# A gated-recurrence and retention layer: the next half's h and the out-projection's tiles loaded into their own slots and split there, and a reordered release of the result banks

## Chip, cores and metric

One NeuronCore of a Trainium2 chip runs the whole layer as one launch. The metric is the device time of one execution in microseconds (us), lower is better; the figure that is compared is the median of several executions.

## Reference

One layer over 2048 positions of width 1024, in float32. All large products are dense; the two mixers are run chunk by chunk.

```
mod = silu(c) @ w_ada + b_ada ;  shift, scale, gate = split(mod)
h    = rms_norm(x, norm_g) * (1 + scale) + shift                     # 2048 x 1024
proj = h @ w_in                                                      # 1024 -> 9216
hq, hf, hi, hz, rq, rk, rv, rz, ga, gb = split(proj)
uA = head_rms_norm(HGRN2(silu(hq), f(hf), hi)) * silu(hz)            # 8 heads of 128
uB = head_rms_norm(Retention(rotary(rq), rotary(rk), rv)) * silu(rz) # 8 heads, key 64, value 128
m  = sigmoid(ga) * uA + sigmoid(gb) * uB
x  = x + gate * (m @ w_out)
out = rms_norm(x, final_g)
```

## The kernel before

The sequence is handled in two halves of 1024 positions (`sb` 0 and 1), each of two blocks of 512 (`tb`). The projection is cut into 72 "quads" (36 for each half, listed in `ORDER`): a quad is 256 columns of w_in for the 1024 positions of a half. A quad is made by seven block products instead of eight (a Strassen form): product `m` = 1 to 7 multiplies one combination of the four 512 x 512 quarters of h (named A11, A12, A22, S1, S2, S3, S4 in `combos`) with one combination of the weights, as 4 steps of three 128x128 by 128x512 matmuls. The three come from a split of each float32 operand into a high part (rounded to fp32r) and the rest: `split_into` lets ScalarE (ACT) copy the source into the first half of a tile and VectorE (DVE) subtract that copy from the source into the second half.

TensorE (PE) runs in the order of the program. `product_order` interleaves quad n = i+1 with the end of quad i: (2,n) (7,i) (1,n) (5,n) (4,i) (3,n) (6,n). Each quad owns one result bank, `x0` or `x1` by its parity; the sums of 2 and 5, 3 go through `y` (in the same bank) and `v`, which ACT copies out (`stash`, lines L477). (4,i) ends a quad, and its result is left in the quad's bank, where `take_a` (a gate's sigmoid, L571), `take_v` (a transpose on DVE, L588), `take_b` (rotary products, L639 to L642) or `take_g` (sigmoid L680 and product L685) read it. Not until they have done so can the product (2, n+1), or the transposes `turned_u` that put the mixers' output in the same bank, begin. `meet` (L703) multiplies the gate with those transposes.

The other engines' order is set by a list scheduler: program order, except that work inside `tc.high_priority(offset=...)` is ranked that many instructions earlier. Each engine then takes its instructions strictly in the order written. All DMAs of the loop but the weights (ACT's queue) and the rotary tables (GpSimd's) are issued by SyncE's queue (SP), also in order.

Tiles and slots that matter here: `tmp` hands out scratch tiles of 128x512 (tag "tp", `NTP` = 4 slots) to everything short-lived. `a_tile` hands out the 28 (`NA`) tiles of tag "A"; in the loop these are the seven combinations of h by four row tiles, and in the last part w_out and m.

Beside the loop runs work in small steps, put between products by `Background`: `tree`, `hgrn_out` and `retention` (the mixers); and, as a side thread that gets a step about once a product, `next_h`. It computes h for the second half (statistics, then x transposed times scale and shift), stores it to memory, loads it back four tiles at a time, forms the four sums (`combine`, L301 to L307, in place) and stores all seven combinations (L1062). At the end of the first half `change_h` loads each combination into a scratch tile (L1072), takes an A tile and splits it. `NEXT` says after which products its steps stand.

At the end `load_wo` loads w_out, multiplies it by the gate (L1244) and splits it into A tiles (L295, L296), `out_m` does the same with m, `meet_last` does the last gate, and `out_half` makes 24 matmuls for 128 positions and 512 columns (`ops`).

Of the kernel before, what the change touches and what calls it, by code (L numbers as in the profile page):

```python
# [32 lines left out]
NBW = 3  # L33
NR = 5
NCC = 5
NTP = 4
NQP = 3
NVH = 2
GAP = 8.0
# [23 lines left out]
def tile_hybrid(ctx: ExitStack, tc: tile.TileContext, a: dict, out: bass.AP):  # L63
# [41 lines left out]
        return t  # L105

    NC = 4 * NBLK
    msk = cpool.tile([P, 4, NC, 16], U8, name="msk", tag="msk")
    dmsk = cpool.tile([P, NC, 2], U8, name="dmsk", tag="dmsk")

    def late_consts():
        m32 = upool.tile([P, 512], I32, name="m32", tag="tp", bufs=NTP)
        nc.sync.dma_start(out=m32[:, 0:66], in_=a["msk"])
        G.tensor_copy(
            out=msk, in_=m32[:, 0:64].rearrange("p (l t) -> p l t", l=4).unsqueeze(2).broadcast_to([P, 4, NC, 16])
        )
# [29 lines left out]

    ng = const("ng", [P, KT], a["ng_t"])
    bad = const("bad", [P, 2 * KT], a["bada_t"])
    lg = const("lg", [P, 2 * H], a["lb_t"])
    lb = cpool.tile([P, H], F32, name="lb", tag="lb")  # L150
    omlb = cpool.tile([P, H], F32, name="omlb", tag="omlb")
    nomlb = cpool.tile([P, H], F32, name="nomlb", tag="nomlb")
# [30 lines left out]

    ad = cpool.tile([P, NC, 32], F32, name="ad", tag="ad")
    G.memset(ad, 0.0)
    junk = cpool.tile([P, P], mybir.dt.bfloat16, name="junk", tag="junk")

    mT_dram = [dram(f"mT{sb}_{b}", [H, P, BLK]) for sb in range(NSB) for b in range(NBLK)]

# [104 lines left out]
    def split_into(t, src):  # L294
        S.activation(out=t[0], in_=src, func=AF.Copy)  # L295
        return V.tensor_tensor(out=t[1], in0=src, in1=t[0], op=ALU.subtract)  # L296

    def combine(h11, h12, h21, h22, use):
        for nm, t in (("A11", h11), ("A12", h12), ("A22", h22)):
# [180 lines left out]
    def after(m, q):  # L480
        with tc.high_priority(offset=PEV):
            if m == 2:
                c2s[q] = stash(f"c2_{q}", yb.pop(q))
                return
            if m == 5:
                c5s[q] = stash(f"c5_{q}", vb[q])
                return
            if m == 1:
                t = c2s.pop(q)
                V.tensor_tensor(out=t, in0=xb[q], in1=t, op=ALU.add)  # L490
                got = (0, 0, t)
            elif m == 3:
                c5s[q, 3] = stash(f"c53_{q}", vb.pop(q))
                return
            elif m == 6:
                t = c5s.pop((q, 3))
                V.tensor_tensor(out=t, in0=t, in1=xb[q], op=ALU.subtract)  # L497
                got = (1, 0, t)
            elif m == 7:
                t = c5s.pop(q)  # L500
                V.tensor_tensor(out=t, in0=t, in1=xb[q], op=ALU.subtract)
                got = (1, 1, t)
            else:
                got = (0, 1, xb.pop(q))
        deliver(q, *got)

    def xtag(q):
# [192 lines left out]
    def meet(sb, h, s, tb, g):  # L700
        b = sb * NBLK + tb
        u = mus.pop((h, s, tb))
        V.scalar_tensor_tensor(  # L703
            out=u, in0=g, scalar=gnt[:, s * H + h : s * H + h + 1], in1=uts.pop((h, s, tb)), op0=ALU.mult, op1=ALU.mult
        )
# [14 lines left out]
    def tree(h, sb, f, k, q):  # L720
# [15 lines left out]
        for li in range(7):  # L736
# [49 lines left out]
                )  # L786
            if m < 16:
                V.copy_predicated(  # L788
                    out=ad.rearrange("p c (n two m) -> p (c n) two m", two=2, m=m)[:, :, 1, :],
                    mask=msk[:, li].rearrange("p c (n m) -> p (c n) m", m=m),  # L790
                    data=ps[:, 0 : 16 * NC].rearrange("p (n m) -> p n m", m=m),
                )
# [29 lines left out]
    def normed(pos, dsts, nm, eps=None):  # L822
        n = len(pos)
        ss = upool.tile([P, 2], F32, name=f"ss{nm}", tag="ss", bufs=4)
        rr = upool.tile([P, 2], F32, name=f"rr{nm}", tag="rr", bufs=4)
        for i in range(n):
            S.activation(out=junk, in_=pos[i], func=AF.Square, accum_out=ss[:, i : i + 1])  # L827
        rstd_of(rr[:, 0:n], ss[:, 0:n], P, eps)
        for i in range(n):
            S.activation(out=dsts[i], in_=pos[i], func=AF.Copy, scale=rr[:, i : i + 1])  # L830
# [188 lines left out]
    def next_h(sb):  # L1019
# [30 lines left out]
                htd[tb, kt] = dram(f"hT{b}_{kt}", [P, 512])  # L1050
                nc.sync.dma_start(out=htd[tb, kt], in_=x)
        for j in range(4):
            hs = []
            for tb, kt in ((0, j), (0, 4 + j), (1, j), (1, 4 + j)):
                hs.append(tmp(f"hT{tb}_{kt}"))
                nc.sync.dma_start(out=hs[-1], in_=htd[tb, kt])
            yield
            yield

            def keep(nm, src):  # L1060
                t = hsd[sb, nm, j] = dram(f"hs{sb}_{nm}_{j}", [P, 512])
                nc.sync.dma_start(out=t, in_=src)  # L1062

            combine(*hs, keep)
            yield
            yield

    def change_h(sb):
        for nm in ("A12", "S1", "A11", "S4", "S2", "S3", "A22"):
            for j in range(4):  # L1070
                x = tmp(f"hl{sb}_{nm}_{j}")
                nc.sync.dma_start(out=x, in_=hsd[sb, nm, j])  # L1072
                t = combos[sb, nm, j] = a_tile(f"{nm}_{sb}_{j}")
                split_into(t, x)
                yield


# [156 lines left out]
    def load_wo():  # L1234
        take("f", 1)
        both = upool.tile([P, 1024], F32, name="gates", tag="f", bufs=1)
        for nh in range(2):
            gate[nh] = both[:, nh * 512 : (nh + 1) * 512]
            nc.sync.dma_start(out=gate[nh], in_=gated[nh])
            for kt in range(KT):  # L1240
                w = tmp(f"wr{kt}_{nh}")
                nc.sync.dma_start(out=w, in_=a["w_o"][kt // 2, nh][:, kt % 2, :])
                t = wod[kt, nh] = a_tile(f"wo{kt}_{nh}")
                V.tensor_tensor(out=w, in0=w, in1=gate[nh], op=ALU.mult)  # L1244
                split_into(t, w)
                yield

    def out_m(t):
        mts[t] = []
        for q4 in range(2):  # L1250
            mr = tmp(f"mr{t}_{q4}")
            nc.sync.dma_start(
                out=mr.rearrange("p (k t) -> p k t", t=P),
                in_=mT_dram[t // 4][4 * q4 : 4 * q4 + 4, :, (t % 4) * P : (t % 4 + 1) * P].rearrange("k p t -> p k t"),
            )
            m = a_tile(f"m{t}_{q4}")
            split_into(m, mr)
            mts[t].append(m)

    def out_half(t, nh):  # L1260
# [4 lines left out]
        xh = [xts[t][:, i * 512 : (i + 1) * 512] for i in range(2)]  # L1265
        ss = sss[t]
        fg = pro["fg"]
        ps = bank(f"ops{t}_{nh}", ("x0", "x1", "v")[pro["n"] % 3])
        pro["n"] += 1
        for kt in range(KT):  # L1270
            hi, lo = mts[t][kt // 4]
# [40 lines left out]
    for i in range(2, len(seq)):  # L1312
# [20 lines left out]
        if q == NQ - 1:  # L1333
            if m == 1:
                pro["w"] = load_wo()
            if m in (1, 3, 6, 7):
                some(pro["w"], {1: 4, 3: 4, 6: 4, 7: 4}[m])
            if m == 4:
                pro["fg"] = apool.tile([P, 1024], F32, name="fg", tag="A", bufs=NA)
                nc.sync.dma_start(out=pro["fg"], in_=a["fg"].broadcast_to([P, 1024]))  # L1340
                V.tensor_scalar(
                    out=pro["fg"], in0=pro["fg"], scalar1=float(D) ** 0.5, scalar2=None, op0=ALU.mult
                )
                out_m(0)
        product(i)

    meet_last()
    pro["n"] = 0
    T0 = 2
    order = [(t, nh) for nh in range(2) for t in range(T0)] + [(t, nh) for t in range(T0, L // P) for nh in range(2)]  # L1350
    nm = 1
    for t, nh in order:
        while nm < min(t + 3, L // P):
            if nm == CH:
                bg.drain()
# [103 lines left out]
```

## Time and profile before

| what | value |
|---|---|
| median of 3 executions | 2226.56 us (2220.96 to 2232.41) |
| the profiled execution | 2225.14 us, its span 2223.3 us |
| granted TensorE clock, mean | 0.95 |
| busy share of the span: PE, PE weight load, DVE, ACT, GpSimd | 90%, 72%, 64%, 45%, 12% |
| moved by DMA | 263.10 MB, 118 GB/s |

The views read below: the list of waits ("engine line <- what released it: us in total, times, longest us"), the timeline (start, duration, engine, line, what is written and read, count; in square brackets how long the engine was idle before, and what ended that), and the chain of work that ended last (start, duration, what). `y L70 <- vt L588` reads: PE stood before a matmul into y until DVE's transpose of line 588 had ended.

### The profile page before, as it was taken

How to read it: one execution, taken by the hardware profiler on the slowest of the kernel's cores; microseconds unless marked ns; L12 is line 12 of the kernel's file. 1: busy time of each engine (PE TensorE's matmuls, PEld its weight loads, DVE VectorE, ACT ScalarE, POOL GpSimd, SP SyncE). 2: the span in 40 equal slices, each digit the busy share in tenths (PEclk: the TensorE clock that was granted, in tenths of full speed). 3: DMA queues.
4: the chain of work that ended last, by engine and by line, in shares of the span. 5: the costliest groups of instructions: out<-in, count | busy, mean ns of one | idle time of the engine just before them, and what ended most of it. 6: DMA issues, size and time to landing. Idle time of an engine off the chain costs nothing.

```text
span 2223.3 us, 40029 instructions
## 1 busy us (share of the span) xinstructions
PE 1998.1 (90%) x15108; PEld 1611.3 (72%) x15108; DVE 1421.4 (64%) x2677; ACT 1002.2 (45%) x2434; POOL 275.5 (12%) x514
## 2 busy tenths in 40 slices
PE   4889899999998688889789899998999899898998
PEld 2667688777776566678668688776777778686887
DVE  5876666676756466656776767665766676568333
ACT  5624445544464353444535444544454345444232
POOL 1002110211021100210001210211021101210000
PEclk8999899999999899989899899999999999899999
DMA  8154424342344437624444424342354423234443
GB/s 282 35 117 120 121 59 118 95 117 78 103 137 135 128 104 211 205 78 126 140 100 122 124 73 104 93 124 85 83 145 124 123 76 103 89 107 152 133 150 115
DMA packets 454849, 263.10 MB, mean 118 GB/s; under 512 B 171905, under 2 KB 406401, under 8 KB 454657
## 3 DMA queue, kind: packets, MB, share of 16 engines
q1 hardware_dynamic: 288480, 176.04, 28.0%
q10 hardware_dynamic: 153120, 76.04, 12.0%
q0 software_dynamic: 13056, 8.47, 1.5%
q8 instruction: 119, 1.95, 0.4%
q14 instruction: 74, 0.60, 0.1%
HBM read 188.03 MB, written 72.35 MB: 117 GB/s over the span
## 4 chain that ended last, share of the span: by engine, by line
PE 40%; DVE 9%; DMA 9%; ACT 4%; issue 3%; POOL 2%; SPq 1%; ACTq 0%; DVEq 0%; POOLq 0%
PE x L70 15%; PE ops L70 8%; PE v L70 8%; PE y L70 4%; DVE b L296 2%; PE poh L70 1%; ACT b L295 1%; DMA w<-in_w_b_dram 1%; PE lv L70 1%; DMA sn<-lin 1%; DMA w<-in_w_d_dram 1%; DVE w L416 1%; PE uT L73 1%; PE rt L70 1%; POOL rrh L177 1%
## 5 line engine op out<-in xcount | busy, mean ns | idle before, releaser
L296 DVE TENSOR_TENSOR b<-w,b 128x512 fp32r<-128x512 f32 (+1 forms) x553 | 346.4, 635 | 328.0 <-ACT b L295 318.2
L295 ACT ACTIVATE b<-w 128x512 fp32r<-128x512 f32 (+1 forms) x553 | 316.7, 583 | 356.9 <-PE x L70 265.9
L70 PE MATMUL v<-S,b 128*128 128x512 f32 x1704 | 432.1, 403 | 20.7 <-ACT c L477 14.1
L70 PE MATMUL x<-A,b 128*128 128x512 f32 x1704 | 430.3, 401 | 5.1 <-ACT c L477 3.8
L70 PE MATMUL x<-S,b 128*128 128x512 f32 x1704 | 433.0, 403 | 0.8 <-DVE c L497 0.8
L70 PEld LDWEIGHTS v<-S,b 128*128 128x128 f32 x1704 | 323.1, 193 | 93.2 <-ACT c L477 16.7
L70 PEld LDWEIGHTS x<-A,b 128*128 128x128 f32 x1704 | 322.5, 192 | 73.8 <-ACT c L477 4.2
L70 PEld LDWEIGHTS x<-S,b 128*128 128x128 f32 x1704 | 322.6, 193 | 67.8 <-DVE c L497 1.2
L70 PE MATMUL y<-A,b 128*128 128x512 f32 x840 | 218.4, 411 | 40.1 <-DVE vt L588 32.3
L416 DVE TENSOR_TENSOR w<-w,w 128x512 f32<-128x512 f32 x284 | 194.7, 686 | 80.3 <-DMA w<-in_w_b_dram 26.8
L70 PEld LDWEIGHTS y<-A,b 128*128 128x128 f32 x840 | 163.1, 198 | 77.0 <-issue 36.1
L70 PE MATMUL ops<-wo,m 128*128 128x512 f32 x768 | 176.3, 392 | 0.0
L70 PEld LDWEIGHTS ops<-wo,m 128*128 128x128 f32 x768 | 145.5, 190 | 30.4
L174 POOL TENSOR_SCALAR ssh<-ssh 128x1 f32<-128x1 f32 x128 | 41.8, 327 | 847.8 <-ACT junk L827 844.6
L477 ACT ACTIVATE c<-v 128x512 f32<-128x512 f32 x142 | 84.3, 594 | 115.7 <-PE v L70 98.3
L70 PEld LDWEIGHTS lv<-q,k 128*32 128x32 f32 (+1 forms) x5888 | 71.9, 111 | 43.7 <-issue 30.2
L830 ACT ACTIVATE uh<-poh,rrh 128x128 f32<-128x128 f32 x128 | 47.1, 368 | 123.3 <-POOL rrh L177 123.3
L497 DVE TENSOR_TENSOR c<-c,x 128x512 f32<-128x512 f32 x71 | 48.7, 686 | 80.7 <-PE x L70 80.3
L70 PE MATMUL lv<-q,k 128*32 128x16 f32 (+2 forms) x5888 | 83.3, 189 | 18.4 <-DVE ad L788 6.4
L776 DVE TENSOR_TENSOR q<-q,f 128x512 f32<-128x512 f32 x112 | 76.8, 685 | 19.6 <-PE lv L70 19.5
L477 ACT ACTIVATE c<-y 128x512 f32<-128x512 f32 x70 | 41.7, 596 | 98.4 <-PE y L70 98.4
L177 POOL TENSOR_TENSOR rrh<-ssh,mhalf 128x1 f32<-128x1 f32 x128 | 82.8, 647 | 10.5
(191 smaller groups left out, 2444.4 us busy)
## 6 DMA issues: line engine op xcount, KB each, us to landing
w<-in_w_d_dram ACTq DMA_DIRECT2D x128, 256.0 KB
w<-in_w_c_dram ACTq DMA_DIRECT2D x66, 256.0 KB
mu<-ud SPq DMA_DIRECT2D x64, 256.0 KB
w<-in_w_a_dram ACTq DMA_DIRECT2D x60, 256.0 KB
wa<-in_w_ada_dram SPq DMA_DIRECT2D x16, 512.0 KB
w<-in_w_b_dram ACTq DMA_DIRECT2D x32, 256.0 KB
vd<-vt SPq DMA_DIRECT2D x128, 64.0 KB
vh<-vd SPq DMA_DIRECT2D x64, 128.0 KB
```

The costliest lines, as they stand in the source:

```text
L70: return tc.keep_in_program_order(nc.tensor.matmul(**kw))
L73: return tc.keep_in_program_order(nc.tensor.transpose(**kw))
L174: G.tensor_scalar(out=ss, in0=ss, scalar1=n * EPS, scalar2=None, op0=ALU.add)
L177: G.tensor_tensor(out=dst, in0=ss, in1=mhalf.broadcast_to([P, w]), op=ALU.pow)
L295: S.activation(out=t[0], in_=src, func=AF.Copy)
L296: return V.tensor_tensor(out=t[1], in0=src, in1=t[0], op=ALU.subtract)
L416: V.tensor_tensor(out=out, in0=x, in1=y, op=ALU.add)
L477: S.activation(out=t, in_=ps, func=AF.Copy)
L497: V.tensor_tensor(out=t, in0=t, in1=xb[q], op=ALU.subtract)
L776: V.tensor_tensor(out=qv, in0=qv, in1=tv[:, :, :, 0:1].broadcast_to([P, NU, nb, m]), op=ALU.mult)
L830: S.activation(out=dsts[i], in_=pos[i], func=AF.Copy, scale=rr[:, i : i + 1])
```

## The change

1. `change_h` and `out_m` load straight into the second half of the A tile (seen as float32) and split there: ACT copies to the first half, DVE subtracts in place (`split_here`). No scratch tile is used, and the DMA now waits for the A tile to be free, in SP's queue.
2. `next_h` no longer stores A11, A12 and A22 again: `change_h` reads them from where h was first stored. The four sums are made one load after another, with two scratch tiles at first and one more for each sum, over 8 steps instead of 4 for each of four groups.
3. `NTP` goes from 4 to 5. The space comes from a mask kept once instead of eight times (`msk`, broadcast when it is read, L788), a bf16 scratch row that is dropped (`junk`; ACT's square of L827 writes the destination tile instead), and a constant that borrows another tile's slot.
4. The reading of (4,i)'s result (`deliver` for m = 4) and the product in `meet` move inside `tc.high_priority`, by 600 instructions.
5. At the end: m's first two tiles are loaded at products 6 and 7 of the last quad rather than at and after product 4; the first `out_half` stands before `meet_last`; the result banks are taken in the order x0, v, x1. `load_wo` takes the A tile before the scratch tile.

```
-NTP = 4
+NTP = 5
...
+    def split_here(t):
+        raw = t[1].bitcast(F32)
+        S.activation(out=t[0], in_=raw, func=AF.Copy)
+        V.tensor_tensor(out=t[1], in0=raw, in1=t[0], op=ALU.subtract)
...
             else:
-                got = (0, 1, xb.pop(q))
+                deliver(q, 0, 1, xb.pop(q))
+                return
         deliver(q, *got)
...
-        V.scalar_tensor_tensor(
-            out=u, in0=g, scalar=gnt[...], in1=uts.pop((h, s, tb)), op0=ALU.mult, op1=ALU.mult
-        )
+        with tc.high_priority(offset=PEV):
+            V.scalar_tensor_tensor(... the same ...)
...
-                    mask=msk[:, li].rearrange("p c (n m) -> p (c n) m", m=m),
+                    mask=msk[:, li].rearrange("p (n m) -> p n m", m=m).unsqueeze(1).broadcast_to([P, NC, 16 // m, m]),
...
-            S.activation(out=junk, in_=pos[i], func=AF.Square, accum_out=ss[:, i : i + 1])
+            S.activation(out=dsts[i], in_=pos[i], func=AF.Square, accum_out=ss[:, i : i + 1])
...
         for j in range(4):                                          # next_h
-            hs = []
-            for tb, kt in ((0, j), (0, 4 + j), (1, j), (1, 4 + j)):
-                hs.append(tmp(f"hT{tb}_{kt}"))
-                nc.sync.dma_start(out=hs[-1], in_=htd[tb, kt])
-            yield
-            yield
...
-            combine(*hs, keep)
+            for nm, at in (("A11", (0, j)), ("A12", (0, 4 + j)), ("A22", (1, 4 + j))):
+                hsd[sb, nm, j] = htd[at]
...
+            h22, h21 = load(1, 4 + j), load(1, j)
             yield
+            yield
+            V.tensor_tensor(out=h22, in0=h21, in1=h22, op=ALU.subtract)
+            keep("S1", h22)
+            h11 = load(0, j)
+            yield
+            yield
+            V.tensor_tensor(out=h21, in0=h11, in1=h21, op=ALU.subtract)
+            keep("S3", h21)
+            V.tensor_tensor(out=h11, in0=h22, in1=h11, op=ALU.subtract)
+            keep("S2", h11)
+            yield
+            h12 = load(0, 4 + j)
+            yield
+            yield
+            V.tensor_tensor(out=h12, in0=h12, in1=h11, op=ALU.add)
+            keep("S4", h12)
             yield
...
-                x = tmp(f"hl{sb}_{nm}_{j}")                         # change_h
-                nc.sync.dma_start(out=x, in_=hsd[sb, nm, j])
                 t = combos[sb, nm, j] = a_tile(f"{nm}_{sb}_{j}")
-                split_into(t, x)
+                nc.sync.dma_start(out=t[1].bitcast(F32), in_=hsd[sb, nm, j])
+                split_here(t)
...
-            mr = tmp(f"mr{t}_{q4}")                                 # out_m
+            m = a_tile(f"m{t}_{q4}")
             nc.sync.dma_start(
-                out=mr.rearrange("p (k t) -> p k t", t=P),
+                out=m[1].bitcast(F32).rearrange("p (k t) -> p k t", t=P),
...
-            m = a_tile(f"m{t}_{q4}")
-            split_into(m, mr)
+            split_here(m)
...
+            if m in (6, 7):
+                out_m(m - 6)
             if m in (1, 3, 6, 7):
-                some(pro["w"], {1: 4, 3: 4, 6: 4, 7: 4}[m])
+                some(pro["w"], 4)
...
-                out_m(0)                                            # was at m == 4
         product(i)
...
-    meet_last()
...
-    nm = 1
+    nm = 2
     for t, nh in order:
+        if (t, nh) == (1, 0):
+            meet_last()
```

What the scheduler makes of it. DVE, where h's sums for the second half are made (`hT`, from L301) and a value tile is transposed out of the bank x (`vt`, reading `x`); before:

```order
L416 TENSOR_TENSOR w_1_8654<-w_1_8654,w_3_8725 128x512
L301 TENSOR_TENSOR hT_4_8642<-hT_0_8640,hT_4_8642 128x512
L303 TENSOR_TENSOR hT_0_8640<-hT_0_8636,hT_0_8640 128x512
L305 TENSOR_TENSOR hT_0_8636<-hT_4_8642,hT_0_8636 128x512
L307 TENSOR_TENSOR hT_4_8638<-hT_4_8638,hT_0_8636 128x512
L588 STREAM_TRANSPOSE vt_7_0_1_8685<-x_8362 128x512
L581 TENSOR_TENSOR q_0_8606<-c_29_8720,sg_0_1_0_8762 128x512
```

The same place on DVE in the changed kernel (L592 is the transpose, L1074 the first sum):

```order
L294 TENSOR_TENSOR b_30_8682<-w_2_8582,b_30_8682 128x512
L592 STREAM_TRANSPOSE vt_7_0_1_8680<-x_8361 128x512
L294 TENSOR_TENSOR b_29_8704<-w_1_8436,b_29_8704 128x512
L1074 TENSOR_TENSOR hT_4_8635<-hT_0_8637,hT_4_8635 128x512
L500 TENSOR_TENSOR c_29_8702<-c_29_8702,x_8578 128x512
```

The transpose moved ahead of the sums, and of the weights' split and the sum before them; the four sums no longer stand in a row.

ACT at the change from the first half to the second (`S_1`, `A_1`: copies of the new combinations; `sz`: sigmoid of the last gate, read from bank x); before:

```order
L295 ACTIVATE S_1_1_10608<-hl_S_1_10606 128x512
L571 ACTIVATE sg_1_0_0_10644<-c_36_10560 128x512
L401 DMA w_3_10739<-in_w_c_dram 128x4x128
L295 ACTIVATE S_1_2_10613<-hl_S_2_10611 128x512
L295 ACTIVATE S_1_3_10618<-hl_S_3_10616 128x512
L573 ACTIVATE f_1_10640<-sg_1_0_0_10644,lb,omlb 128x512
L576 ACTIVATE k_1_10641<-sg_1_0_0_10644,omlb,nomlb 128x512
L295 ACTIVATE A_1_0_10668<-hl_A_0_10666 128x512
L680 ACTIVATE sz_7_1_10708<-x_10368 128x512
```

And now:

```order
L298 ACTIVATE S_1_3_10568<-S_1_3_10568 128x512
L404 DMA w_2_10576<-in_w_c_dram 128x4x128
L575 ACTIVATE sg_1_0_0_10595<-c_36_10519 128x512
L404 DMA w_0_10639<-in_w_c_dram 128x4x128
L480 ACTIVATE c_36_10615<-v_10599 128x512
L293 ACTIVATE b_36_10633<-w_0_10385 128x512
L577 ACTIVATE f_1_10591<-sg_1_0_0_10595,lb,omlb 128x512
L580 ACTIVATE k_1_10592<-sg_1_0_0_10595,omlb,nomlb 128x512
L684 ACTIVATE sz_7_1_10655<-x_10339 128x512
L293 ACTIVATE b_37_10659<-w_2_10576 128x512
L298 ACTIVATE A_1_0_10617<-A_1_0_10617 128x512
```

All copies of the S combinations now stand ahead of the copy of the result bank v (L480), and `sz` stands ahead of the first copy of A22.

PE at the end of the last quad (`uT` are the transposes of `meet_last`, `ops` the out-projection); before:

```order
L70 MATMUL x_20116<-A_1_3_10683,b_71_20253 128x512 x3
L73 MATMUL uT_0_1_20341<-ident,mu_7_3_20088 128x128 x4
L70 MATMUL ops_0_20371<-wo_0_20094,m_0_20316 128x512 x3
L70 MATMUL ops_0_20371<-wo_0_20100,m_0_20316 128x512 x3
L70 MATMUL ops_0_20371<-wo_0_20106,m_0_20316 128x512 x3
```

And now, after eight rows of `ops_0_20305` (24 matmuls), of which the last three are shown:

```order
L70 MATMUL ops_0_20305<-wo_0_20129,m_1_20179 128x512 x3
L70 MATMUL ops_0_20305<-wo_0_20135,m_1_20179 128x512 x3
L70 MATMUL ops_0_20305<-wo_0_20141,m_1_20179 128x512 x3
L73 MATMUL uT_0_1_20334<-ident,mu_7_3_20035 128x128 x4
L70 MATMUL ops_0_20352<-wo_0_20039,m_0_20228 128x512 x3
```

One block of the out-projection passed the transposes; everything else on PE stands as before.

More of the change, by code (lines that the diff above doesn't have):

```diff
@@ L107, in tile_hybrid @@
     NC = 4 * NBLK
-    msk = cpool.tile([P, 4, NC, 16], U8, name="msk", tag="msk")
+    msk = cpool.tile([P, 4, 16], U8, name="msk", tag="msk")
     dmsk = cpool.tile([P, NC, 2], U8, name="dmsk", tag="dmsk")
@@ L113, in late_consts @@
         nc.sync.dma_start(out=m32[:, 0:66], in_=a["msk"])
-        G.tensor_copy(
-            out=msk, in_=m32[:, 0:64].rearrange("p (l t) -> p l t", l=4).unsqueeze(2).broadcast_to([P, 4, NC, 16])
-        )
+        G.tensor_copy(out=msk, in_=m32[:, 0:64].rearrange("p (l t) -> p l t", l=4))
         G.tensor_copy(out=dmsk, in_=m32[:, 64:66].unsqueeze(1).broadcast_to([P, NC, 2]))
@@ L148, in tile_hybrid @@
     bad = const("bad", [P, 2 * KT], a["bada_t"])
-    lg = const("lg", [P, 2 * H], a["lb_t"])
+    lg = upool.tile([P, 256], F32, name="lg", tag="dT", bufs=1)[:, 0 : 2 * H]
+    nc.sync.dma_start(out=lg, in_=a["lb_t"])
     lb = cpool.tile([P, H], F32, name="lb", tag="lb")
@@ L185, in tile_hybrid @@
     G.memset(ad, 0.0)
-    junk = cpool.tile([P, P], mybir.dt.bfloat16, name="junk", tag="junk")
     mT_dram = [dram(f"mT{sb}_{b}", [H, P, BLK]) for sb in range(NSB) for b in range(NBLK)]
@@ L702, in meet @@
         u = mus.pop((h, s, tb))
-        V.scalar_tensor_tensor(
-            out=u, in0=g, scalar=gnt[:, s * H + h : s * H + h + 1], in1=uts.pop((h, s, tb)), op0=ALU.mult, op1=ALU.mult
-        )
+        with tc.high_priority(offset=PEV):
+            V.scalar_tensor_tensor(
+                out=u, in0=g, scalar=gnt[:, s * H + h : s * H + h + 1], in1=uts.pop((h, s, tb)), op0=ALU.mult,
+                op1=ALU.mult,
+            )
         if (h, b) not in half:
@@ L788, in tree @@
                 V.copy_predicated(
-                    out=ad.rearrange("p c (n two m) -> p (c n) two m", two=2, m=m)[:, :, 1, :],
-                    mask=msk[:, li].rearrange("p c (n m) -> p (c n) m", m=m),
-                    data=ps[:, 0 : 16 * NC].rearrange("p (n m) -> p n m", m=m),
+                    out=ad.rearrange("p c (n two m) -> p c n two m", two=2, m=m)[:, :, :, 1, :],
+                    mask=msk[:, li].rearrange("p (n m) -> p n m", m=m).unsqueeze(1).broadcast_to([P, NC, 16 // m, m]),
+                    data=ps[:, 0 : 16 * NC].rearrange("p (c n m) -> p c n m", c=NC, m=m),
                 )
@@ L1052, in next_h, with load @@
         for j in range(4):
-            hs = []
-            for tb, kt in ((0, j), (0, 4 + j), (1, j), (1, 4 + j)):
-                hs.append(tmp(f"hT{tb}_{kt}"))
-                nc.sync.dma_start(out=hs[-1], in_=htd[tb, kt])
-            yield
-            yield
+            for nm, at in (("A11", (0, j)), ("A12", (0, 4 + j)), ("A22", (1, 4 + j))):
+                hsd[sb, nm, j] = htd[at]
+            def load(tb, kt):
+                x = tmp(f"hT{tb}_{kt}")
+                nc.sync.dma_start(out=x, in_=htd[tb, kt])
+                return x
             def keep(nm, src):
@@ L1240, in load_wo @@
             for kt in range(KT):
+                t = wod[kt, nh] = a_tile(f"wo{kt}_{nh}")
                 w = tmp(f"wr{kt}_{nh}")
                 nc.sync.dma_start(out=w, in_=a["w_o"][kt // 2, nh][:, kt % 2, :])
-                t = wod[kt, nh] = a_tile(f"wo{kt}_{nh}")
                 V.tensor_tensor(out=w, in0=w, in1=gate[nh], op=ALU.mult)
@@ L1267, in out_half @@
         fg = pro["fg"]
-        ps = bank(f"ops{t}_{nh}", ("x0", "x1", "v")[pro["n"] % 3])
+        ps = bank(f"ops{t}_{nh}", ("x0", "v", "x1")[pro["n"] % 3])
         pro["n"] += 1
```

## The prediction

> **What bounds the kernel now.** I read the page first, then PE's list of waits, then the timeline at each long wait, and the chain for what follows a wait.
>
> ```profile
> span 2223.3 us, 40029 instructions
> PE 1998.1 (90%) x15108; PEld 1611.3 (72%) x15108; DVE 1421.4 (64%) x2677; ACT 1002.2 (45%) x2434; POOL 275.5 (12%) x514
> ```
>
> PE is the bound: it is idle for 2223.3 - 1998.1 = 225 us in all, and the change leaves its instructions as they are but for one block at the end. So the change is worth what it takes from, or adds to, that idle time. The list of waits says what ends it:
>
> ```profile
> PE y L70 <- DVE vt L588: 32.3, 4, 10.1
> PE uT L73 <- DVE sz L685: 22.7, 6, 9.6
> PE uT L73 <- ACT c L477: 22.6, 16, 3.0
> ...
> PE v L70 <- ACT c L477: 14.1, 8, 5.2
> ...
> PE rb L70 <- POOL dgr L1037: 9.9, 3, 5.1
> ...
> PE y L70 <- ACT sg L571: 6.1, 1, 6.1
> ...
> PE v L70 <- DVE mu L703: 2.6, 1, 2.6
> ...
> PE y L70 <- DVE ro L641: 1.6, 1, 1.6
> ```
>
> Five of these rows (vt, sz, sg, mu, ro) are the reading of (4,i)'s bank or `meet`, which the change ranks earlier: 32.3 + 22.7 + 6.1 + 2.6 + 1.6 = 65.3 us in 13 waits. The rest (c, rb and smaller) it does not aim at. Where the long ones stand, from PE's timeline:
>
> ```profile
> 134.21 2.04 PE L70 MATMUL y<-A,b 128*128 128x512 f32 x4 [10.11 <-DVE vt L588]
> ...
> 730.48 4.31 PE L70 MATMUL y<-A,b 128*128 128x512 f32 x12 [9.23 <-DVE vt L588]
> ...
> 879.39 2.05 PE L70 MATMUL y<-A,b 128*128 128x512 f32 x4 [9.42 <-DVE vt L588]
> ...
> 913.32 5.03 PE L70 MATMUL y<-A,b 128*128 128x512 f32 x12 [6.10 <-ACT sg L571]
> ...
> 1092.85 1.11 PE L73 MATMUL uT<-ident,mu 128*128 128x128 f32 x4 [9.55 <-DVE sz L685]
> ...
> 1733.95 2.47 PE L70 MATMUL y<-A,b 128*128 128x512 f32 x5 [3.58 <-DVE vt L588]
> ...
> 2039.20 1.11 PE L73 MATMUL uT<-ident,mu 128*128 128x128 f32 x4 [8.20 <-DVE sz L685]
> ```
>
> A wait costs more than its length. The chain shows the twelve matmuls just after one, and twelve in full run:
>
> ```profile
> 879.39 4.91 PE y L70 x12
> 884.30 2.75 PE x L70 x12
> ...
> 1072.04 5.47 PE v L70 x12
> ```
>
> After the 9.42 us wait they took 4.91 us instead of 2.75: 2.2 us extra, which I take behind the other long waits too. The slow twelve at 1072.04 follow the single mu wait of 2.6 us, so a short one can cost as much.
>
> **The change, wait by wait.** At 879 the bank was not waiting for a late product but for DVE's place in line and a scratch tile:
>
> ```profile
> 872.96 0.69 DVE L301 TENSOR_TENSOR hT<-hT,hT 128x512 f32<-128x512 f32 x1
> ...
> 878.53 0.72 DVE L588 STREAM_TRANSPOSE vt<-x 128x512 f32<-128x512 f32 x1 [2.71 <-DMA hs_S<-hT]
> ```
>
> The transpose stood behind the four sums of h (the first is the row at 872.96) and then 2.71 us for a store of one of them. (4,i) had ended two products earlier, so in the new order, ahead of the sums and with a fifth scratch tile, it can run during those products. I take the whole 9.4 us, and 2.2 behind it: 11.6. At 913 the sigmoid of (4,i) stood behind a DVE chain that the same stores held up:
>
> ```profile
> 908.94 0.69 DVE L301 TENSOR_TENSOR hT<-hT,hT 128x512 f32<-128x512 f32 x1 [3.70 <-DMA hs_A<-hT]
> ...
> 912.67 0.60 ACT L571 ACTIVATE sg<-x 128x512 f32<-128x512 f32 x1 [1.78 <-DVE hT L305]
> ```
>
> The `hs_A` stores are gone (12 of 256 KB; the sums overwrite nothing that is being stored), and `sg` stands some dozen ACT rows earlier: 6.1 + (5.03 - 2.75) = 8.4.
>
> At 1092 ACT came late to the sigmoid:
>
> ```profile
> 1083.70 0.63 ACT L295 ACTIVATE S<-hl_S 128x512 fp32r<-128x512 f32 x1 [1.41 <-DMA hl_S<-hs_S]
> ...
> 1090.09 0.63 ACT L295 ACTIVATE A<-hl_A 128x512 fp32r<-128x512 f32 x1 [0.78 <-DMA hl_A<-hs_A]
> 1091.47 0.60 ACT L680 ACTIVATE sz<-x 128x512 f32<-128x512 f32 x1 [0.76 <-DVE A L296]
> ```
>
> PE had finished the last product before the wait at 1092.85 - 9.55 = 1083.3, and bank x one product earlier; `sz` stood behind loads and copies of the new combinations. It now stands ahead of A22's copies, and the S copies stand earlier: 9.5 + 2.2 = 11.7.
>
> At 2039, the end of the loop, PE stands 8.20 us for the last `sz`. A block of 24 matmuls now comes first (5.5 us at 2.75 for 12), if its operands are there:
>
> ```profile
> 2014.37 18.12 SPq L1242 DMA_DIRECT2D wr<-in_w_o_dram  x10
> ...
> 2027.78 1.29 DVE L296 TENSOR_TENSOR wo<-wr,wo 128x512 fp32r<-128x512 f32 x2
> ...
> 2035.77 1.58 SPq L1252 DMA_DIRECT2D mr<-mT  x2
> ...
> 2041.39 0.63 ACT L295 ACTIVATE m<-mr 128x512 fp32r<-128x512 f32 x1 [1.75 <-DMA mr<-mT]
> ```
>
> The eighth w_out tile, the last that the block needs, is split at 2028.5. m's loads stand last in SP's queue before; they now stand behind ten of the sixteen w_out loads. Loads come at some 18.12 / 10 = 1.8 us, so the six fewer put them about 11 us earlier, near 2025, and with the 5.6 us from the first issue to the second tile's copy (2035.77 to 2041.39) m is there about 2030.6, just before PE ends at 2039.20 - 8.20 = 2031.0. I take 8.2 + 2.2 = 10.4.
>
> At 730:
>
> ```profile
> 721.81 0.68 DVE L497 TENSOR_TENSOR c<-c,x 128x512 f32<-128x512 f32 x1
> ...
> 729.62 0.71 DVE L588 STREAM_TRANSPOSE vt<-x 128x512 f32<-128x512 f32 x1
> ```
>
> The transpose now follows the sum of L497 directly, which itself needs the product that ends at 730.48 - 9.23 = 721.25. It ends at 722.49 + 0.71 = 723.2, so 2 us of wait stay: 7.2 saved, and of the slow twelve behind (4.31 - 2.75 = 1.6) half: 8.0. At 1733.95 it stands ahead of that sum but behind w_gate's work: 2.5 of 3.58, and 1 behind it: 3.5. At 134 little changes, since DVE stands for a weight load there and the transpose still comes seven rows after it:
>
> ```profile
> 128.62 0.69 DVE L416 TENSOR_TENSOR w<-w,w 128x512 f32<-128x512 f32 x1 [1.98 <-DMA w<-in_w_c_dram]
> ```
>
> I take 0.8. The six that are left (four short sz waits, 22.7 - 9.55 - 8.20 = 4.95, ro and mu) are 9.2 us; half: 4.6.
>
> Sum: 11.6 + 8.4 + 11.7 + 10.4 + 8.0 + 3.5 + 0.8 + 4.6 = 59.0 us.
>
> **What it gives back.** While PE stands, DVE and ACT catch up; without the stand they meet PE later with that work undone. The c waits of L477 are of this kind: (22.6 + 14.1) / 24 = 1.5 us each. I put two such behind each of the five long waits that go: 15 us. Bounds: nothing, if DVE at 64% and ACT at 45% absorb it, or half of the sum, 29.5 us.
>
> **Parts costed at nothing.** The square of L827 writes f32 to its destination instead of bf16:
>
> ```profile
> L830 ACT ACTIVATE uh<-poh,rrh 128x128 f32<-128x128 f32 x128 | 47.1, 368 | 123.3 <-POOL rrh L177 123.3
> L827 ACT ACTIVATE junk<-poh 128x128 bf16<-128x128 f32 x128 | 35.3, 276 | 55.8 <-DVE st L900 45.1 <-DVE st L898 8.9 <-issue 0.2
> ```
>
> Between 0 and 368 - 276 = 92 ns for each of 256 squares is 0 to 24 us of ACT, hidden by ACT's 55% idle time; I take 0, as both read PSUM and the scaled copy has an operand more. The broadcast mask leaves L788's element count alone: 0 to 6 us of DVE (64 x 0.1), beside other work. Twelve stores fewer, 3 of 263 MB, and a side thread that ends 16 steps later: at one step a product, 16 x 2.75 = 44 us behind its last sums, which puts it some 100 us ahead of the landing at 1082.65 below, where they are read. In-place splits cost as much as before: same engines, shapes and counts.
>
> The SP queue is where a cost could come from: 28 loads now wait there for an A tile. A group of four is issued at 2.96 / 4 = 0.74 us each, and the landing on the chain took 3.24 us:
>
> ```profile
> 1086.69 2.96 SPq L1072 DMA_DIRECT2D hl_A<-hs_A  x4
> ...
> 1082.65 3.24 DMA hl_S<-hs_S
> ...
> 1703.19 11.13 DMA w<-in_w_b_dram
> ```
>
> The fourth is there 3 x 0.74 + 3.24 = 5.5 us after the product that frees the tiles; the copies of y and v that ACT makes behind such a split have two products, also 5.5 us, before PE misses them. So nothing, but with no margin: rival (d). Behind these loads in SP's queue stand only m's stores, which nobody reads until the end.
>
> 59 - 15 = 44 us: 2225.1 - 44 = 2181 for a profiled execution. That execution stands 1.4 us under the median of the runs, so the median comes to **2183 us**.
>
> The Trainium skill's page "TensorE: Matmul & The Clock Gate", section "Part 1: The HAM clock gate", says that PE drops to half its clock after about 3.4 us of idleness and needs about 3.4 us of work to return. The twelve slow matmuls after 9.42 us agree; those after the 2.6 us wait do not, so the trace has no such safe length. An estimate by that page: each of the six waits over 3.4 us that go or shrink gives back 1.7 us, 10.2 in all, where my rows have 2.2 + 2.3 + 2.2 + 2.2 + 0.8 + 1 = 10.7, so the sum would be 0.5 us less.
>
> **Rivals.** (a) Full relief: nothing is given back and the fifth scratch tile also ends the rb waits (9.9): 2226.6 - 59 - 10 = 2158. For it: DVE and ACT are far from full; against: around the longest waits DVE has little to spare, 42.91 of 60 us:
>
> ```profile
> 1050.00:1110.00 60.00, 47.17 (x187) 37.65 (x186) 42.91 (x68) 30.89 (x55) 0.80 (x1) 0.86 0.49 150
> ```
>
>  (b) Waits handed on: half the sum, and 7 us more at the next weights' splits that have been pushed behind: 2226.6 - 22 = 2204. For it: that row of DVE. (c) The change does not do what it says: the early rows wait for scratch tiles that are no sooner free, so only the end is gained, 2226.6 - 8 = 2219. For it: the 2.71 us above was a tile's wait; against: a fifth tile, and the stores of A11, A12, A22 that held them are gone. (d) Slower: SP's loads land too late, ACT stands before the copies of y and v, and PE behind it, seven times. With a landing of L us each costs 2.2 + L - 5.5 plus 2.2 for slow matmuls; seven eat up 44 us from L = 7.4 on, and with the 11.13 us of the slowest load shown they cost 7 x 10.0 = 70: 2183 + 70 = 2253. Against: the landing of 3.24.
>
> **Chances.** The forecast (2170 to 2196) 0.62, (a) 0.13, (b) 0.12, (c) 0.08, (d) 0.05. The range leaves out (c), (d) and what lies beyond (a): 2156 to 2214. A change of under 0.5% (11 us, about the spread of the three runs shown) can't be told from none: faster than 2215.4 by forecast, (a) and (b) 0.87, the same by (c) 0.08, slower by (d) 0.05.
>
> **What would show it.** In the changed kernel's list of waits, vt under 15 us (mainly the one near 134), sz under 5, no sg; the c waits of L477 grow from 37 to some 45 to 55. At the end PE goes from the last product into `ops` without a wait over 1 us. Wrong if new PE waits on A or S splits stand between 1000 and 1070, if `vt` waits on DMA as before, or if the waits of weights' splits (b) grow by more than 25 us.

## Result, and the profile after

The changed kernel takes 2156.77 us (median of 4 runs, 2149.55 to 2160.67) against 2227.49 us before: a ratio of 0.9681 with a 95% interval of 0.9644 to 0.9717, or 71 us. The profiled execution has a span of 2154.3 us, 69.0 less than before. Its page, of the kernel after (busy time, share of the span, instructions):

```profile
span 2154.3 us, 40023 instructions
PE 1978.3 (92%) x15108; PEld 1598.5 (74%) x15108; DVE 1416.6 (66%) x2677; ACT 995.0 (46%) x2434; POOL 278.5 (13%) x514
```

The 69.0 us are two things. PE's idle time fell from 225.2 to 2154.3 - 1978.3 = 176.0 us, by 49.2; and the same 15108 matmuls took 1998.1 - 1978.3 = 19.8 us less, since fewer of them ran slowly just behind a wait (the mean granted clock rose from 0.950 to 0.966; the last section shows the rows).

The list of waits of PE, after:

```profile
PE uT L73 <- ACT c L480: 30.1, 20, 4.5
...
PE x L70 <- ACT c L480: 12.2, 4, 5.9
...
PE rb L70 <- POOL dgr L1043: 9.2, 2, 6.2
PE y L70 <- DVE vt L592: 8.6, 2, 7.1
...
PE v L70 <- ACT c L480: 6.0, 6, 1.8
PE gps L70 <- DVE acc L1246: 4.8, 1, 4.8
...
PE uT L73 <- DVE sz L689: 0.7, 3, 0.3
```

`vt` went from 32.3 to 8.6 us, `sz` from 22.7 to 0.7, and `sg`, `mu` and `ro` are gone. The copies `c` stand at 30.1 + 12.2 + 6.0 = 48.3 us against 22.6 + 14.1 + 3.8 (their waits before an x matmul) = 40.5 before; the two rows of them that the prediction counted went from 36.7 to 36.1, so what grew is the waits before x matmuls. The `gps` wait is new. The places that the prediction walked through, in PE's timeline after, with DVE's transpose for the second of them:

```profile
716.93 3.00 PE L70 MATMUL y<-A,b 128*128 128x512 f32 x12 [1.50 <-DVE vt L592]
...
855.50 2.98 PE L70 MATMUL y<-A,b 128*128 128x512 f32 x12
...
881.24 2.88 PE L70 MATMUL y<-A,b 128*128 128x512 f32 x12
...
1045.93 0.66 PE L73 MATMUL uT<-ident,mu 128*128 128x128 f32 x4 [0.25 <-DVE sz L689]
...
1666.89 2.88 PE L70 MATMUL y<-A,b 128*128 128x512 f32 x12
...
1971.95 5.61 PE L70 MATMUL ops<-wo,m 128*128 128x512 f32 x24
1977.40 0.60 PE L73 MATMUL uT<-ident,mu 128*128 128x128 f32 x4
```

```profile
850.69 0.71 DVE L592 STREAM_TRANSPOSE vt<-x 128x512 f32<-128x512 f32 x1
...
854.15 0.68 DVE L1074 TENSOR_TENSOR hT<-hT,hT 128x512 f32<-128x512 f32 x1
```

The transpose is done at 851.4, four microseconds before PE needs the bank, and the sums of h come behind it. The groups of twelve shown take 2.9 to 3.0 us; before, the same four took 4.3 to 5.0.

PE's instructions are the same up to the last block, so the start of the same matmul in both traces gives a ledger (its sum, 69.3 us, runs to the last matmul; a second trace of the changed kernel differs from it by up to 2.2 us in a stretch):

| stretch of the kernel before (us) | what stands there | change in the stretch |
|---|---|---|
| 0 to 205 | start, vt at 134 | +0.7 |
| 205 to 688 | c at 498 (-7.4 there, 4.4 given back behind it) | -3.0 |
| 688 to 812 | vt at 730 | -11.8 |
| 812 to 939 | vt at 879, sg at 913 | -19.4 |
| 939 to 1131 | mu at 1072, sz at 1092 | -20.0 |
| 1131 to 1487 | | +1.2 |
| 1487 to 1683 | c at 1508 | -6.3 |
| 1683 to 1956 | vt at 1734 (-8, and 7 given back, mostly to gps) | -1.0 |
| 1956 to 2078 | the end of the loop | -9.7 |

### The profile page after: what moved, and what is told of

It reads as the page before. It is cut to its first block, busy times and chain, and to the rows that moved or that the text cites. A ratio compares the mean times of both kernels' runs of the same rounds, so it can differ in the third digit from the quotient of the medians.

```text
span 2154.3 us, 40023 instructions
## 1 busy us (share of the span) xinstructions
PE 1978.3 (92%) x15108; PEld 1598.5 (74%) x15108; DVE 1416.6 (66%) x2677; ACT 995.0 (46%) x2434; POOL 278.5 (13%) x514
## 4 chain that ended last, share of the span: by engine, by line
PE 43%; DVE 7%; DMA 5%; ACT 4%; POOL 2%; issue 2%; ACTq 0%; SPq 0%; POOLq 0%; DVEq 0%
PE x L70 16%; PE v L70 8%; PE ops L70 8%; PE y L70 3%; DVE b L294 2%; PE lv L70 2%; PE poh L70 2%; PE rt L70 1%; DMA w<-in_w_d_dram 1%; ACT b L293 1%; DVE w L419 1%; PE uT L73 1%; PE por L70 1%; POOL rrh L176 1%; ACT c L480 1%
## 5 line engine op out<-in xcount | busy, mean ns | idle before, releaser
L70 PE MATMUL y<-A,b 128*128 128x512 f32 x840 | 209.1, 398 | 8.6 <-DVE vt L592 8.6
L70 PEld LDWEIGHTS y<-A,b 128*128 128x128 f32 x840 | 156.9, 190 | 41.8 <-issue 7.4
L480 ACT ACTIVATE c<-v 128x512 f32<-128x512 f32 x142 | 84.5, 595 | 121.7 <-PE v L70 106.9
L70 PE MATMUL lv<-q,k 128*32 128x16 f32 (+2 forms) x5888 | 82.5, 189 | 18.9 <-DVE ad L794 6.2
L782 DVE TENSOR_TENSOR q<-q,f 128x512 f32<-128x512 f32 x112 | 76.9, 687 | 22.6 <-PE lv L70 22.2
L176 POOL TENSOR_TENSOR rrh<-ssh,mhalf 128x1 f32<-128x1 f32 x128 | 84.0, 656 | 10.4
L783 DVE TENSOR_TENSOR k<-k,f 128x512 f32<-128x512 f32 x112 | 77.1, 688 | 0.0
```

What stands on the lines that cost most here:

```text
L70: return tc.keep_in_program_order(nc.tensor.matmul(**kw))
L176: G.tensor_tensor(out=dst, in0=ss, in1=mhalf.broadcast_to([P, w]), op=ALU.pow)
L480: S.activation(out=t, in_=ps, func=AF.Copy)
L782: V.tensor_tensor(out=qv, in0=qv, in1=tv[:, :, :, 0:1].broadcast_to([P, NU, nb, m]), op=ALU.mult)
L783: V.tensor_tensor(out=kv, in0=kv, in1=tv[:, :, :, 1:2].broadcast_to([P, NU, nb, m]), op=ALU.mult)
```

## Experiments

The two theories. "Order": the rank of part 4 is what brought the bank's release forward. "Tiles": a reading of the bank needs a scratch tile, and the scheduler can't write it earlier than a tile comes free; then whatever frees tiles helps, and the rank little. Parts 1 and 2 (for h), 3 and 4 were taken alone on the kernel before; these (of part 3 the tile) and the order of part 5 were undone in the changed one. Part 1's loads of m were not tested by themselves.

**Part 4 alone, and the changed kernel without it.** On the kernel before:

```
-                got = (0, 1, xb.pop(q))
+                deliver(q, 0, 1, xb.pop(q))
+                return
...
+        with tc.high_priority(offset=PEV):      # meet
```

> The kernel before with part 4 alone: the reading of (4,i)'s bank and the product in meet ranked 600 earlier; four scratch tiles, the 12 stores and the old tail stay. Theory 'order': the bank's release stood too late in DVE's and ACT's lines, and the order cures it by itself. Then the waits at 730 (8.0), 879 (11.7 with the slow matmuls), 1092 (12) and the small ones (5 to 8) go, the tail's 10 and 913's share of the stores stay: 2227 - 35 to 45, so 2182 to 2192, vt in the list of waits under 15 us. Rival 'tiles': the transposes and sigmoids that are ranked earlier must take a scratch tile out of four, three of which h's stores hold; they stand in DVE's line until those are stored, and so does all behind them: 2227 - 0 to 15, vt still over 20 us and now on a DMA.

> The changed kernel without part 4: (4,i) and meet in program order; loads into own slots, five scratch tiles and the new tail stay. Theory 'order': the waits of 730, 879 (but for the 2.7 us of a store), 1092 and the small ones come back: 2157 + 30 to 45, so 2187 to 2202, vt 20 to 30 us, sz 10 to 15. Rival 'tiles': the gain was that nothing stands on scratch tiles and stores any more: 2157 + 0 to 15, vt under 15 us.

Alone it came to 2217.29 us (ratio 0.9959, 0.9945 to 0.9973): 8 us. Without it the changed kernel took 2172.78 (0.9762, 0.974 to 0.9785), so it is worth 16 us there (18 by each session's kernel before), and 53 to 55 of the 71 us come without it. That is just outside what "tiles" gave (up to 2172), with vt at 10.4 us as it said; sz came to 17.3 us, for which "order" had 10 to 15. The trace of part 4 alone, DVE and then PE at the place that was at 879:

```profile
873.80 0.69 DVE L301 TENSOR_TENSOR hT<-hT,hT 128x512 f32<-128x512 f32 x1 [1.96 <-DMA ud<-uh]
...
877.38 0.72 DVE L589 STREAM_TRANSPOSE vt<-x 128x512 f32<-128x512 f32 x1 [0.70 <-DMA hs_S<-hT]
```

```profile
878.24 4.84 PE L70 MATMUL y<-A,b 128*128 128x512 f32 x12 [9.38 <-DVE vt L589]
```

Ranked 600 earlier, the transpose stands just where it stood: behind the four sums, waiting for one of their stores, and PE waits 9.38 us. "Order" falls for this place, and "tiles" had it right. Where the rank does count, with the other parts in place, is at the change of halves and at the end; PE in the changed kernel without it:

```profile
1058.92 1.12 PE L73 MATMUL uT<-ident,mu 128*128 128x128 f32 x4 [4.88 <-DVE sz L688]
...
1993.03 1.12 PE L73 MATMUL uT<-ident,mu 128*128 128x128 f32 x4 [6.22 <-DVE sz L688]
```

**One tile fewer.** The changed kernel with `NTP = 4`.

> The changed kernel with NTP = 4 instead of 5, all else as it is. Theory 'order': one tile fewer delays some early rows by a product's time now and then: 2157 + 0 to 10. Rival 'tiles': the fifth tile is what lets the early rows run; without it vt and sz wait for a tile: 2157 + 20 to 40, so 2177 to 2197.

2177.91 us (0.9787, 0.9764 to 0.9809), 21 us slower: the lower end of "tiles". PE's waits:

```profile
PE uT L73 <- ACT c L480: 28.4, 20, 4.4
PE y L70 <- DVE vt L592: 18.8, 2, 9.7
...
PE v L70 <- ACT c L480: 13.4, 9, 5.2
```

The long `vt` at 730 is back, and so are the `c` waits of over 3 us at 498 and 1508. 879 stayed away: with four tiles too, the new loads clear it, as their own run below shows.

**Part 3 alone, and its control.** On the kernel before, the space savings with `NTP = 5`, and, as a control, the same savings with `NTP = 4` kept:

```
-NTP = 4
+NTP = 5
...
-    msk = cpool.tile([P, 4, NC, 16], U8, name="msk", tag="msk")
+    msk = cpool.tile([P, 4, 16], U8, name="msk", tag="msk")
```

> The kernel before with part 3 alone: a fifth scratch tile and the space that pays for it (one mask instead of eight, no scratch row for the squares). Theory 'tiles': what the changed kernel lost with four tiles comes here as a gain, at 730 (8), 498 and 1508 (5 each), 1734 (4): 2226 - 12 to 22; the waits at 879, 913 and 1092 stay, since h's sums still fill five tiles as they filled four: vt still over 15 us, sz over 15. Rival 'any tile will do': a fifth tile also frees the rows behind h's sums: 2226 - 35 or more. That the squares in float32 and the broadcast mask cost time would show here as ACT or DVE busy time over 1002 and 1421 us: I expect no more than 3 us of either.

> The control of the run with part 3 alone (2181): the same space savings, the float32 squares and the broadcast mask, but NTP = 4 again, so the space gained is left unused. If the fifth tile made that run's 44 us, this one is the kernel before: 2225 +- 6. If the savings themselves did something (a lighter mask, a write less), 2210 or below; if they cost something that the tile covered up, 2232 or above.

2180.74 us (0.9793, 0.9772 to 0.9815): 44 of the 71 us from the fifth tile and its space, without any rank, without the new loads, with the old tail. The control took 2217.92 (0.9964, 0.9952 to 0.9977), so the tile itself is worth 37 us and the savings some 9. I had put 879 and 913 down as staying; "any tile will do", with its 35 or more, was right. With part 3 alone, at the same two products:

```profile
854.21 0.71 DVE L586 STREAM_TRANSPOSE vt<-x 128x512 f32<-128x512 f32 x1
```

```profile
855.57 2.98 PE L70 MATMUL y<-A,b 128*128 128x512 f32 x12
```

The traces show the same move in DVE's order. In the kernel before, the transpose is the 1112th of DVE's 2677 instructions, right behind the four sums (1108th to 1111th), and so it is in the control and with part 4 alone. With part 3 alone it is the 1103rd, and the first sum the 1111th. So the move that the order showed at 879 was the tile's. Of the control's 9 us no single place has more than 1.6; ACT was busy 998.0 us and DVE 1422.9, so the float32 squares and the broadcast mask cost nothing that shows. What made the 9 stays open; the 8 us of the rank alone are no more than that.

**The loads, alone and undone.** Parts 1 and 2 for h on the kernel before, and the changed kernel with h's old stores and loads:

```
-                x = tmp(f"hl{sb}_{nm}_{j}")
-                nc.sync.dma_start(out=x, in_=hsd[sb, nm, j])
                 t = combos[sb, nm, j] = a_tile(f"{nm}_{sb}_{j}")
-                split_into(t, x)
+                nc.sync.dma_start(out=t[1].bitcast(F32), in_=hsd[sb, nm, j])
+                split_here(t)
```

> The kernel before with parts 1 and 2 for h alone: the combinations load into their own A tiles and are split there, the twelve stores are gone, the sums are made one load after another; four scratch tiles, the old order of (4,i) and the old tail stay. Theory 'tiles' (a reading of the bank takes a scratch tile, and the tiles were held by h's sums and stores and by the new half's loads): 879 (11.7 us), 913 (8.5) and 1092 (12, with a further 7 to 10 around it) are relieved and the waits at 730, 498, 1508, 1734 stay: 2226 - 30 to 40, so 2186 to 2196. Rival 'only together': without the fifth tile and the earlier order the same rows find no tile: 2226 - 5 to 15.

> The changed kernel with next_h and change_h as before: h's sums in groups of four with all seven combinations stored, and each loaded to a scratch tile and split from there; five tiles, the order and the new tail stay. Theory 'tiles': 879, 913 and 1092 come back though the rows are ranked early: 2157 + 25 to 40, so 2182 to 2197. Theory 'order': early rows and a fifth tile do without it: 2157 + 0 to 12.

Alone: 2203.29 us (0.9898, 0.9879 to 0.9917), 21 us, between the two expectations: 879 and 913 go, as they do by the tile alone (the transpose is DVE's 1102nd instruction), but the change of halves gives 4.9 us where 19 to 22 were reckoned. Undone in the changed kernel: 2161.96 (0.9716, 0.9694 to 0.9738), a loss of 5 us only, which the intervals do not separate from none. The range is the one given for "order", but what clears 879 and 913 there is the tile. PE waits 7.01 us for a load of the retention's rows near 873 instead, as it does with part 3 alone (7.06), and 7.31 us for `sz` at the change of halves, and gets about half of that back behind them. PE's wait for `sz` in that run:

```profile
PE uT L73 <- DVE sz L689: 7.6, 2, 7.3
```

So the fifth tile and the loads are in part two cures of one illness: 37 and 21 us alone, but taken from the full change 21 and 5.

**The end.** The changed kernel with `meet_last` again ahead of the out-projection, m's first tiles at product 4 and after it, and the banks in the old order:

```
-            if m in (6, 7):
-                out_m(m - 6)
...
+    meet_last()
     pro["n"] = 0
```

> The changed kernel with part 5's order undone: meet_last before the out-projection, m's first tiles loaded at product 4 and after it, the banks in the old order. Both theories: the last wait comes back, sz about 8 us and 2 us of slow matmuls behind it: 2157 + 8 to 10.5, so 2165 to 2168. If the gain at the end belongs to the other parts (the last sz earlier through part 4, m not behind a scratch tile), then 2157 + 0 to 4.

2161.41 us (0.971, 0.9688 to 0.9733), 5 us slower than the changed kernel by the medians, though the intervals overlap; it lies between the two ranges that were expected. PE at the end of the loop in that run:

```profile
1971.82 1.11 PE L73 MATMUL uT<-ident,mu 128*128 128x128 f32 x4 [3.58 <-DVE sz L689]
...
1977.54 1.22 PE L70 MATMUL ops<-wo,m 128*128 128x512 f32 x2 [4.62 <-ACT m L298]
```

The wait for `sz` was down from 8.20 to 3.58 us (8.67 with part 4 alone, so the rank needs other parts for it), but m came 4.62 us late: together 8.20 again. In this trace the loop's end takes 12.0 us longer than in the changed kernel's, more than the 9.7 us gained there; how much of it the total keeps is not clear, with 5 us between the medians.

**Place by place.** The ledger above, for each run's trace, in us against the kernel before:

| kernel | 688 to 812 (730) | 812 to 939 (879, 913) | 939 to 1131 (change of halves) | 1956 to 2078 (end) |
|---|---|---|---|---|
| changed | -11.8 | -19.4 | -20.0 | -9.7 |
| part 4 alone | -4.9 | -0.1 | -4.9 | +1.1 |
| parts 1, 2 for h alone | +0.3 | -18.9 | -4.9 | +0.1 |
| part 3 alone | -14.5 | -10.0 | -11.2 | +0.1 |
| changed without part 4 | -11.2 | -18.3 | -7.1 | -1.4 |
| changed with the old loads of h | -14.1 | -10.0 | -14.5 | -9.7 |
| changed with four tiles | -7.7 | -19.0 | -17.4 | -7.2 |
| changed with the old end | -10.9 | -19.4 | -16.9 | +2.3 |

So 879 and 913 are the tile's or the loads', and the rank has no share there that shows. No part alone cures the change of halves, and it loses most without the rank. At the end the rank and part 5 gain next to nothing without each other.

**Whether more is to be had.** The waits on `c` are the longest left, so the rank was raised for all of `after` (`PEV = 1200`, `PEV = 2000`), and a sixth tile was paid for with two buffers of the retention's rows:

```
-NTP = 5
+NTP = 6
...
-    u[j] = upool.tile([P, 2, P], F32, name=..., tag="ur", bufs=4)
+    u[j] = upool.tile([P, 2, P], F32, name=..., tag="ur", bufs=2)
```

> The changed kernel with PEV = 1200 instead of 600: the copies of y and v, the sums of 1, 6 and 7 and the reading of (4,i) ranked twice as early. The largest waits left are those on the copies (c, 48.3 us in 30 waits); at 527, 913 and 1480 the copy of v stands on ACT behind the scaling of the mixers' output, which waits for GpSimd. If the rank sets that, the copies pass it and 10 to 25 us go: 2132 to 2147. If the copies are already as early as their products allow, or what passes them is only something else late: 2157 +- 5. If what is ranked earlier blocks ACT or DVE while it waits for its product: 2162 to 2180.

> The changed kernel with PEV = 2000, after 1200 came out 6 us under the changed kernel's earlier figure with the waits on the copies of y and v as long as before (46.3 against 48.3 us). If those 6 us are the rank's doing, it holds or grows: 2140 to 2152. If they were the scatter between chips and runs, it equals the run beside it within 5 us. If rank begins to block engines: over 2162.

> The changed kernel with a sixth scratch tile, paid for by two buffers fewer of the retention's output rows (ur, 4 to 2). Theory 'tiles' says that with four the bank's readings had no tile (21 us over the changed kernel): if five are still short, six bring some 5 to 15 us more, in vt at 136 and c: 2142 to 2152. If five were enough, nothing: 2157 +- 5; and if the two missing buffers hold up the retention, it shows as waits on ur and 2162 or more.

> The changed kernel once more, as the reference on this chip for the two runs beside it: 2157 +- 5.

`PEV = 1200`: 2150.94 us (0.966, 0.9638 to 0.9683). In another session the changed kernel again took 2155.87 (0.9677, 0.9654 to 0.97), `PEV = 2000` 2153.20 (0.9673, 0.965 to 0.9696) and six tiles 2156.42 (0.9692, 0.967 to 0.9714). All four intervals overlap: none of these beats the changed kernel by what can be measured. `PEV = 1200` came out just under its range of no effect (2152 to 2162), and `PEV = 2000` within 3 us of the run beside it, so those few us were scatter. With six tiles the list of waits reads

```profile
PE uT L73 <- ACT c L480: 29.3, 20, 3.9
...
PE x L70 <- ACT c L480: 14.1, 4, 7.7
...
PE rt L70 <- ACT ur L836: 10.2, 5, 3.3
...
PE y L70 <- DVE vt L592: 5.2, 2, 3.7
```

so `vt` gains 3.4 us (8.6 to 5.2), and the rb waits 3.5 (9.2 to 5.7), but the `c` waits before an x matmul and those on `ur` grow by 1.9 and 0.9, the rest goes in small waits, and the total stays: a sixth tile, bought in this way, brings nothing. What holds `c` is on ACT, shown here in the changed kernel ahead of its 4.46 us wait at 913:

```profile
910.76 0.37 ACT L836 ACTIVATE ur<-por,rrr 128x128 f32<-128x128 f32 x1 [1.34 <-POOL rrr L176]
...
912.42 0.37 ACT L836 ACTIVATE uh<-poh,rrh 128x128 f32<-128x128 f32 x1 [1.03 <-POOL rrh L176]
912.68 0.59 ACT L480 ACTIVATE c<-v 128x512 f32<-128x512 f32 x1
```

The copy stands behind two scalings that wait for GpSimd, and no rank tried here brought the total down by what can be measured.

| kernel | median us | against before (us) |
|---|---|---|
| changed | 2156.8 | -71 |
| part 4 alone / changed without it | 2217.3 / 2172.8 | -8 / -53 |
| parts 1, 2 for h alone / changed without them | 2203.3 / 2162.0 | -21 / -63 |
| part 3 alone / its control with four tiles | 2180.7 / 2217.9 | -44 / -9 |
| changed with four tiles | 2177.9 | -47 |
| changed without part 5's order | 2161.4 | -64 |

## Why the prediction was right or wrong

Right: that PE's idle time decides, that the waits it named would go, and that slow matmuls would go with them; vt under 15 us, sz under 5, no sg and an end without a wait came as said. The measured 2156.8 is 26 us under the forecast of 2183 and outside the 2170 to 2196 that had a chance of 0.62. It lies in the whole range by 0.8 us, at rival (a)'s 2158, and that is luck, since (a)'s road was not taken: the rb waits stayed (9.9 to 9.2 us) and waits did grow elsewhere.

By its terms, against the ledger: 879 and 913 were put at 11.6 + 8.4 = 20.0 and gave 19.4; 730 at 8.0 and gave 11.8 with the waits around it; the end at 10.4 and gave 9.7; 1734 at 3.5 and gave 8 on the spot, of which 7 went again within 60 us; 134 at 0.8, and nothing is left of its 3.0 by 205. The change of halves was put at 11.7 and a part of the 4.6 for small waits, and gave 20.0: behind the 9.3 us of `sz` also went the mu wait of 2.56, 4.0 of the 5.90 us wait at 1130 and two slow stretches.

Three steps failed. First, **the sum of what is gained was too small**: the waits named hold 59.0 - 10.7 = 48.3 us of idle time, but all waits that shrank in the trace (counting differences over 0.05 us at the same matmul) shrank by 91.3. The `c` waits at 498 and 1508, 3.82 and 5.18 us, were taken as part of a kind that only grows; the first fell to 1.01 and the second to nothing, and the run with four tiles has them back (3.55 and 5.19). Second, **what it gives back was mis-sized**, 15 us against 41.8 us of waits that grew, of which only 7.8 in the sum of `c`. Net, idle time fell by 49.2 us where 48.3 - 15 = 33.3 was forecast. Third, **the slow matmuls** were put at 10.7 us and gave 19.8, mostly because places that it gave no price (498, 1072, 1508) had them too, 6.6 us by their rows. The two differences, 15.9 and 9.1 us, are the 25 us that the forecast of 44 lacked. Two smaller slips changed nothing: rival (c) prices the end at 8 us where the sum has 10.4, and the 0.1 us for each copy with the broadcast mask is given without a row (the copy took 363 ns in the median before and 364 after).

**The cause was read wrongly.** The step for 879 says "in the new order, ahead of the sums and with a fifth scratch tile", as if the rank made the order; that for 913 credits the stores that are gone. The runs show that the rank moves nothing at 879 by itself, and that the waits at both places go by the fifth tile alone, with all the stores in place, or by the new loads alone. Those take away stores and loads in fours together, so the stores' own share is not shown. The row of 2.71 us, a transpose that waits for a store, had said so: the tile was the obstacle, and the transpose's place in DVE's line its mark. Rival (c) named this mechanism, but as a reason why the change might do nothing.

By the estimate made from the Trainium skill's page "TensorE: Matmul & The Clock Gate", section "Part 1: The HAM clock gate", the sum would have been 0.5 us less. The traces have slow stretches behind shorter waits than its 3.4 us, from about 1.8 us on (last section). The miss of 9.1 us in the slow matmuls lies mostly in places that were not priced, not in the length of one slow stretch.

Of the parts costed at nothing, the squares and the mask cost nothing (the squares took 275 ns against 276). Rival (d) was there in small: SP's loads did land late, and once that reached PE by (d)'s road. The chain of the changed kernel has

```profile
1018.13 6.60 DMA A<-hT
1028.69 4.58 DMA S<-hs_S
```

against the 3.24 us reckoned with. The copy of v stands on ACT behind the split of that tile of A, and PE waits for the copy:

```profile
1024.76 0.63 ACT L298 ACTIVATE A<-A 128x512 fp32r<-128x512 f32 x1 [0.30 <-DMA A<-hT]
1025.29 0.58 ACT L480 ACTIVATE c<-v 128x512 f32<-128x512 f32 x1
```

```profile
1025.92 0.66 PE L73 MATMUL uT<-ident,mu 128*128 128x128 f32 x4 [1.27 <-ACT c L480]
```

Before, the same matmul waited 0.25 us, so the late loads cost about 1 us here. Between 1000 and 1070 the list of waits has no wait of PE on a split of h itself, and no other over 0.3 us.

## What to carry to other kernels

When an instruction stands late in a list scheduler's order, ask first what it must have, a slot above all, before ranking it earlier: a rank moves only what is free to move, and here one more scratch tile was worth 37 us, where the rank alone was worth 8, no more than the unexplained 9 of the space savings. Cures that free the same resource don't add: runs of each part alone and left out (37 and 21 us here against 21 and 5) show it, a sum over places can't. A long wait of the engine that bounds the kernel is worth its length and the slow stretch behind it, also where it is one of many of a kind.

## What the runs showed of the hardware

The slow stretch behind a wait is one at half the granted clock. In all fourteen traces, these are the rows of twelve 128x512 matmuls behind a wait of PE of 0.8 us or more:

| wait before (us) | rows | twelve matmuls took (us) | granted clock over them |
|---|---|---|---|
| 0.82 to 1.81 | 77 of 78 | 2.97 to 3.06 | 1.00 |
| 1.88 to 10.11 | 53 of 55 | 4.30 to 5.49 | 0.50 to 0.68 |

The three others: 4.61 us behind a wait of 1.80, 2.97 behind 3.00 and 3.00 behind 3.29. Two rows, from before and after, of the same place:

```profile
498.41 5.49 PE L70 MATMUL v<-S,b 128*128 128x512 f32 x12 [3.82 <-ACT c L477]
```

```profile
495.36 3.06 PE L70 MATMUL v<-S,b 128*128 128x512 f32 x12 [1.01 <-ACT c L480]
```

The wait got 2.81 us shorter and the matmuls behind it 2.43. The granted clock over the first row is 0.50, over the second 1.00.

That the length behind a long wait varies without following the wait's (4.91 us behind 9.42, 5.47 behind 2.56) is in the clock records: over these two rows the clock was 0.58 and 0.50, and it came back to 1.0 within the first. In every trace the clock is 1.0 or 0.5, and each such stretch but the last lasts 3.41 us or a multiple of it. This suggests that it matters how a wait falls on these steps: with the steps counted on from their neighbours, the waits of 3.00 and 3.29 us with no slow stretch behind them lay across one, as 1.21 + 1.79 and 1.44 + 1.84 us. What decides between waits of about 1.80 us is not shown here.
